# Linear attention with a relu feature map: the output product computed transposed, and turned back in fp32

## The chip, the cores and the metric

One core of a Trainium2 chip. The metric is the device time of the kernel in microseconds (us), the median of several runs. Smaller is better. All runs that are compared here were in the same (fast) state, with one exception that is named. Most runs of one kernel agree within about 0.3% (within 0.6% at most, but for one kernel that is named), so differences of half a per cent are read from five rounds with an interval.

TensorE is the matrix engine, VectorE and ScalarE work elementwise, GpSimd (POOL in the profile) and SyncE (SP) here mostly issue transfers. PE is TensorE's matmul part and PEld its weight loads, DVE is VectorE, ACT is ScalarE.

## The reference

```python
batch, heads, seq, dim = 8, 12, 512, 64          # Q, K, V: fp32
Q_feat = np.maximum(0, Q);  K_feat = np.maximum(0, K)
KV    = np.einsum('bhkd,bhkv->bhdv', K_feat, V)
K_sum = np.sum(K_feat, axis=2)
numerator   = np.einsum('bhqd,bhdv->bhqv', Q_feat, KV)
denominator = np.einsum('bhqd,bhd->bhq', Q_feat, K_sum)
return numerator / (denominator[:, :, :, None] + 1e-10)
```

There are 96 heads. The kernel takes K and V in 24 groups of four heads and Q in 12 octets of eight heads. A partition holds 16 (K, V) or 32 (Q, out) consecutive rows of 64 numbers, so every transfer of the body is contiguous. It must read 37.75 MB and write 12.58 MB.

## The kernel before

```python
def mm_kv(g):                       # KV and K_sum of one group: 16 matmuls
    ps_kv[g] = pkv.tile([P, 2, D1], fp32, name="ps_kv")
    for r in range(R):
        nc.tensor.matmul(ps_kv[g], kf[g][:, r, :, :]..., vo[g % NB][:, r, :, :], start=(r == 0), ...)

def evac_qt(o, i, eng=None):        # relu(q), transposed; written so that pairs of heads lie 32 columns apart
    for z in range(2):
        ... nc.scalar.activation(qtz[o % NZ][:, z, us, :, z, :], pv[:, :, :, z, :], Act.Relu)

def mm_out(o, j):                   # 128 small matmuls an octet: 32 columns of q as weights, 130 columns of KV
    ...                             # po: a PSUM tile for nu blocks of 128 rows, from block u0
    for v in range(nu):
        u, b, c = u0 + v, v // (nu // 2), v % (nu // 2) * 2 * D1
        for z in range(2):
            for w in range(4):
                hs, h = slice(32 * w, 32 * w + 32), 2 * w + z
                nc.tensor.matmul(po[hs, b, c:c + 2 * D1],
                    qtf[o % NZ][:, z, u * P + 32 * w:u * P + 32 * w + 32],
                    kvd[...][:, h % 4 // 2, h % 2, :, :], start=(z == 0), stop=(z == 1), ...)

def norm(o, j, o_sb):               # the denominator comes as column 64 of each row of the product
    ...                             # pv: a view of the product in PSUM; den and rec: small tiles
    nc.vector.tensor_scalar(den, pv[:, :, :, D], scalar1=1e-10, scalar2=None, op0=Alu.add)
    nc.vector.reciprocal(rec, den)
    nc.vector.tensor_tensor(o_sb[...], pv[:, :, :, 0:D], rec..., op=Alu.mult)

def cuts(o):                        # stores 1 and 3 are cut, so that engines 0 to 4 get more rows
    return ((16, P), (0, 5), (5, 10), (10, 15), (15, 16)) if o in (1, 3) else ((0, P),)

def store(o, o_sb):
    if o + DELAY < NO:              # hold store o back until K of a later octet has landed
        nc.sync.dma_start(out=scratch, in_=k_sb[2 * (o + DELAY)][0:1, 0, :])
    if o == NO - 1: ...             # the last octet's output in two halves
    for p0, p1 in cuts(o):
        nc.sync.dma_start(out=Ov[p0:p1], in_=o_sb[p0:p1])
# ... loads of Q, K, V are issued from GpSimd's queue and cast fp32 to bf16
```

## Time and profile before

| | before |
|---|---|
| time, median of 3 runs | 127.53 us (127.42 to 127.59) |
| span of the profiled run | 125.6 us |
| TensorE matmuls, weight loads | 2112, 2112 |
| last Q landed | 111.5 us |
| last store issued, landed | 119.9, 124.7 us |

Two more views of the kernel before matter later, though the prediction passed them by. The first is the list of transfer queues (queue and kind: packets, MB, and the time that its packets took as a share of the time of all 16 engines). The second lists what TensorE waited for (engine, tile and line, releaser: us in total, times, longest).

```profile
q0 software_dynamic: 8064, 17.83, 74.3%
q1 hardware_dynamic: 2416, 13.63, 27.1%
...
q8 instruction: 16, 0.26, 0.7%
```
```profile
PE ps_out L178 <- issue: 12.4, 7, 3.3
```

The first line of queues is the loads, the second the stores. The third is the program itself. Sixteen packets of 16 KB were read to feed instructions, and they went through the same DMA engines as the data. By the trace's packet records each took 0.88 to 0.98 us of one engine (0.94 us on average); their share of the time agrees (0.7% of 125.6 us, for 16 packets on 16 engines). The wait line is the other side of it: seven times TensorE stood for up to 3.3 us in the output product with no data to wait for. Three more such waits stand in TensorE's other lines. All ten (17.7 us together) end 1.2 to 1.5 us after one of these packets has been read, so they are waits for instructions.

### The profile page before, as it was taken

To read this page: it belongs to the slowest core of one execution; us is meant where nothing else is said; L and a number is where in the kernel's file an instruction comes from. 1 tells how busy PE (TensorE), PEld (TensorE's weight loads), DVE (VectorE), ACT (ScalarE), POOL (GpSimd) and SP (SyncE) were. 2 spreads that over 40 slices of the span, in tenths; PEclk is the share of its full clock that TensorE was granted. 3 is DMA by queue.
4 is the path that set the end of the run, shared out by engine and by line. 5 is a ranking of instruction groups with operands and counts; after the bars stand their busy time and mean duration, and the time that the engine had idled before them with its cause. 6 is when DMAs were issued, how large, how long until landed. Compare 5 with 4: busy or idle time off the path is not lost.

```text
span 125.6 us, 4876 instructions
## 1 busy us (share of the span) xinstructions
PE 78.7 (63%) x2112; PEld 69.4 (55%) x2112; DVE 81.2 (65%) x212; ACT 76.0 (61%) x167; POOL 31.7 (25%) x62
## 2 busy tenths in 40 slices
PE   0042908978398956535996697289765997558300
PEld 0041907957387845435985686287744895457200
DVE  3356785798936959674569697439628658942910
ACT  0255891599298898660899849509908959535000
POOL 6903334323243331241142133034022000000000
PEclk9999999999859999996799859959996579985995
DMA  3999999999999999999999999999999999999993
GB/s 120 378 305 210 217 204 211 217 207 219 202 215 211 208 217 320 260 216 311 270 211 296 290 211 281 296 221 231 343 223 215 328 258 213 322 419 417 407 400 153
DMA packets 10789, 32.82 MB, mean 261 GB/s; under 512 B 1424, under 2 KB 1424, under 8 KB 9360
## 3 DMA queue, kind: packets, MB, share of 16 engines
q0 software_dynamic: 8064, 17.83, 74.3%
q1 hardware_dynamic: 2416, 13.63, 27.1%
q10 hardware_dynamic: 288, 1.05, 2.1%
q8 instruction: 16, 0.26, 0.7%
q14 instruction: 5, 0.04, 0.1%
HBM read 37.75 MB, written 12.58 MB: 401 GB/s over the span
## 4 chain that ended last, share of the span: by engine, by line
DMA 32%; PE 30%; DVE 15%; issue 12%; ACT 6%; SPq 0%; ACTq 0%
DMA v_sb<-in_V_dram 25%; PE ps_out L178 14%; PE ps_kv L139 12%; DMA kv_first<-in_K_dram 7%; DVE o_sb L191 5%; PE ps_qt L153 4%; DVE kf L128 3%; DVE qt L121 3%; ACT qt L163 3%; ACT kvd L146 2%; DVE vo L130 2%; DVE rec L190 1%; ACT vo L134 1%; DVE den L188 1%; DVE kvd L118 0%
## 5 line engine op out<-in xcount | busy, mean ns | idle before, releaser
L139 PE MATMUL ps_kv<-vo,kf 128*128 128x130 bf16 x384 | 33.6, 253 | 22.2 <-ACT vo L134 10.1
L178 PE MATMUL ps_out<-kvd,qt 128*32 128x130 bf16 x1536 | 33.4, 240 | 16.1 <-issue 12.4
L139 PEld LDWEIGHTS <-kf 128*128 128x128 bf16 x384 | 28.6, 114 | 25.6 <-DVE vo L130 16.9
L178 PEld LDWEIGHTS <-qt 128*32 128x32 bf16 x1536 | 26.6, 106 | 21.6 <-issue 14.0
L146 ACT CAST kvd<-ps_kv 64x130 bf16<-64x130 f32 x96 | 25.2, 263 | 19.2 <-PE ps_kv L139 17.3
L134 ACT ACTIVATE vo<-v_sb,mask 128x1024 bf16<-128x1024 bf16 x22 | 26.2, 1190 | 10.9 <-DMA v_sb<-in_V_dram 10.7
L191 DVE TENSOR_TENSOR o_sb<-ps_out,rec 128x768 f32<-128x768 f32 (+1 forms) x36 | 31.3, 869 | 1.4
L163 ACT ACTIVATE qt<-ps_qt 128x512 bf16<-128x512 bf16 x46 | 23.8, 603 | 0.3
L128 DVE TENSOR_SCALAR kf<-k_sb,mask 128x1024 bf16<-128x1024 bf16 x44 | 19.1, 477 | 6.2 <-DMA k_sb<-in_K_dram 6.2
L85 POOL DMA_DIRECT2D k_sb<-in_K_dram x22 | 12.5, 569 | 39.5 <-DMA q_sb<-in_Q_dram 24.6
L188 DVE TENSOR_SCALAR den<-ps_out 128x12 f32<-128x12 f32 (+1 forms) x36 | 5.9, 164 | 17.8 <-PE ps_out L178 17.8
L153 PE MATMUL ps_qt<-ident,q_sb 128*128 128x128 bf16 x192 | 16.3, 251 | 1.2 <-issue 0.9
L87 POOL DMA_DIRECT2D v_sb<-in_V_dram x22 | 12.2, 555 | 16.3 <-DMA k_sb<-in_K_dram 6.7
L153 PEld LDWEIGHTS <-q_sb 128*128 128x128 bf16 x192 | 14.6, 116 | 1.4 <-issue 1.0
L130 DVE TENSOR_SCALAR vo<-v_sb,mask 128x1024 bf16<-128x1024 bf16 x22 | 10.7, 485 | 1.1 <-DMA v_sb<-in_V_dram 1.1
L190 DVE RECIPROCAL rec<-den 128x12 f32<-128x12 f32 (+1 forms) x36 | 7.9, 220 | 1.2
L91 POOL DMA_DIRECT2D q_sb<-in_Q_dram x12 | 6.5, 542 | 7.8 <-DMA v_sb<-in_V_dram 4.1
L128 DVE TENSOR_SCALAR kf<-kv_first,mask 128x1024 bf16<-128x1024 f32 x4 | 2.9, 766 | 4.6 <-DMA kv_first<-in_K_dram 4.6
L134 ACT ACT_TABLE_LOAD x1 | 1.3, 1283 | 5.5 <-DMA kv_first<-in_V_dram 5.5
L121 DVE MEMSET qt<- 128x2048 f32 x2 | 3.5, 1765 | 0.7 <-issue 0.7
L134 ACT ACTIVATE vo<-kv_first,mask 128x1024 bf16<-128x1024 f32 x2 | 2.4, 1179 | 2.7 <-DMA kv_first<-in_V_dram 2.7
L160 DVE TENSOR_SCALAR qt<-ps_qt 128x512 bf16<-128x512 bf16 x2 | 0.8, 420 | 2.9 <-PE ps_qt L153 2.9
(13 smaller groups left out, 4.9 us busy)
## 6 DMA issues: line engine op xcount, KB each, us to landing
out_dram<-o_sb SPq DMA_DIRECT2D x9, 1024.0 KB, 9.4
q_sb<-in_Q_dram POOLq DMA_DIRECT2D x12, 512.0 KB, 14.7
k_sb<-in_K_dram POOLq DMA_DIRECT2D x22, 256.0 KB, 14.0
v_sb<-in_V_dram POOLq DMA_DIRECT2D x22, 256.0 KB, 13.4
out_dram<-o_sb SPq DMA_DIRECT2D x2, 896.0 KB, 8.8
kv_first<-in_V_dram ACTq DMA_DIRECT2D x2, 512.0 KB
kv_first<-in_K_dram SPq DMA_DIRECT2D x2, 512.0 KB
out_dram<-o_sb SPq DMA_DIRECT2D x2, 512.0 KB, 4.7
```

What stands on the lines that cost most here:

```text
L85: nc.gpsimd.dma_start(out=k_sb[g].rearrange("p r d -> p (r d)"), in_=Kr[g])
L87: nc.gpsimd.dma_start(out=v_sb[g].rearrange("p r d -> p (r d)"), in_=Vr[g])
L128: nc.vector.tensor_scalar(kf[g][:, :, s, :], k_sb[g], scalar1=0.0, scalar2=mask[:, 0, s:s + 1], op0=Alu.max, op1=Alu.mult)
L130: nc.vector.tensor_scalar(vo[g % NB][:, :, 0, 0:D], v_sb[g], scalar1=mask[:, 1, 0:1], scalar2=None, op0=Alu.mult)
L134: nc.scalar.activation(vo[g % NB][:, :, 1, 0:D], v_sb[g], Act.Copy, scale=mask[:, 1, 1:2])
L139: nc.tensor.matmul(ps_kv[g], kf[g][:, r, :, :].rearrange("p s d -> p (s d)"), vo[g % NB][:, r, :, :], start=(r == 0), stop=(r == R - 1), s ...
L146: nc.scalar.copy(kvd[g % NK][64 * c:64 * c + 64, :, s, c, :], ps_kv[g][64 * s:64 * s + 64])
L153: nc.tensor.transpose(ps_qt[o, i][:, u, :], q_sb[o][:, i * (U // 2) + u, :], ident)
L163: nc.scalar.activation(qtz[o % NZ][:, z, us, :, z, :], pv[:, :, :, z, :], Act.Relu)
L178: nc.tensor.matmul(po[hs, b, c:c + 2 * D1], qtf[o % NZ][:, z, u * P + 32 * w:u * P + 32 * w + 32], kvd[(2 * o + h // 4) % NK][:, h % 4 // ...
L190: nc.vector.reciprocal(rec, den)
L191: nc.vector.tensor_tensor(o_sb[:, 2 * u0:2 * (u0 + nu)].rearrange("p (b r) d -> p b r d", b=2), pv[:, :, :, 0:D], rec.unsqueeze(3).to_broa ...
```

## The change

The intent is fewer and larger instructions. The output product is computed the other way round (KV as weights, q as the moving operand), eight matmuls of 256 columns in place of 128 small ones. That yields the output transposed. ScalarE (in the last octet VectorE too) copies it out of PSUM in fp32, and TensorE transposes it back in fp32. The denominators get 16 small matmuls of their own. Stores are no longer cut.

```diff
+    def out_t(o):
+        ...                             # q: relu(q), transposed, by heads
+        for j in range(2):
+            ps = pou.tile([P, 4, U, 16], fp32, name="ps_ot", tag="ps_out")
+            for i in range(4):
+                h = 4 * j + i
+                nc.tensor.matmul(ps[:, i], kvd[o % NK][:, h, 1:2 * D + 1], q[:, :, h, :], ...)
+            copy = nc.vector.tensor_copy if o == NO - 1 and j == 1 else nc.scalar.copy
+            copy(ot[o][:, :, 4 * j:4 * j + 4], ps.rearrange("p h u c -> p u h c"))
+    def denom(o):
+        ...                             # ps, own, den: tiles
+        for u in range(U):
+            nc.tensor.matmul(ps[:, u], qt_sb[o % NZ][:, u, :], kvd[o % NK][:, :, 0:2 * D1:2 * D1 - 1], ...)
+        nc.vector.scalar_tensor_tensor(own..., ps..., 1e-10, mask_h..., op0=Alu.add, op1=Alu.mult)
+        nc.vector.tensor_reduce(out=den..., in_=own..., op=Alu.add, ...)
+        nc.vector.reciprocal(rec[o], den)
+    def back(o, j):
+        for v in range(8):
+            nc.tensor.transpose(ps[:, 2 * v:2 * v + 2]..., ot[o][:, 8 * j + v]..., ident32)
+    def norm(o, j, ps, o_sb):
+        nc.vector.tensor_tensor(o_sb[:, rs], ps, rec[o][:, rs]..., op=Alu.mult)
-    def mm_out(o, j):  ...              # and the old norm
-        for p0, p1 in cuts(o):
-            nc.sync.dma_start(out=Ov[p0:p1], in_=o_sb[p0:p1])
+        nc.sync.dma_start(out=Ov, in_=o_sb)
     ... (half of the value copies move from ScalarE to VectorE, K/V of two groups share one
          evacuation, tiles and program order follow; mask_h is summed from the fp32 identity)
```

More of the change, by code (lines that the diff above doesn't have):

```diff
@@ L49 @@
     kfp = pool("kfp", 4)
-    rcp = pool("rcp", 4)
+    rcp = pool("rcp", 2)
     outp = pool("outp", DELAY + 2)
-    pkv = pool("pkv", 2, space=bass.MemoryType.PSUM)
+    otp = pool("otp", 2)
+    pkv = pool("pkv", 1, space=bass.MemoryType.PSUM)
     pqt = pool("pqt", 2, space=bass.MemoryType.PSUM)
+    pde = pool("pde", 1, space=bass.MemoryType.PSUM)
     pou = pool("pou", 2, space=bass.MemoryType.PSUM)
@@ L61 @@
     ident = consts.tile([P, P], bf16, name="ident")
+    ident32 = consts.tile([P, P], fp32, name="ident32")
     NB = 4
-    NK = 4
+    NK = 2
     NZ = 2
-    vo = [consts.tile([P, R, 2, D1], bf16, name=f"vo{i}") for i in range(NB)]
-    kvf = [consts.tile([P, NHG * 2 * D1], bf16, name=f"kvd{i}") for i in range(NK)]
-    kvd = [x.rearrange("p (t s c d) -> p t s c d", t=2, s=2, c=2) for x in kvf]
+    D4 = D + 4
+    vo = [consts.tile([P, R, 2, D4], bf16, name=f"vo{i}") for i in range(NB)]
+    kvf = [consts.tile([P, 8 * 2 * D1], bf16, name=f"kvd{i}") for i in range(NK)]
+    kvd = [x.rearrange("p (h d) -> p h d", h=8) for x in kvf]
     mask = consts.tile([P, 2, 2], fp32, name="mask")
     scratch = consts.tile([1, D], bf16, name="scratch")
-    qtf = [consts.tile([P, 2, U * P], bf16, name=f"qt{i}") for i in range(NZ)]
-    qtz = [x.rearrange("p z (u w y c) -> p z u w y c", u=U, w=4, y=2) for x in qtf]
+    mask_h = consts.tile([P, 8, 2], fp32, name="mask_h")
+    qt_sb = [consts.tile([P, U, P], bf16, name=f"qt{i}") for i in range(NZ)]
+    ps_kv = pkv.tile([P, 2, 256], fp32, name="ps_kv")
     ctx.enter_context(tc.manual_schedule())
@@ L113, in zero, with zero_kv @@
                 nc.vector.memset(mask[64 * t:64 * t + 64, 1, t:t + 1], 1.0)
-        if i < NB:
-            nc.vector.memset(vo[i][:, :, :, D:D1], 0.0)
-            for t in range(2):
-                nc.vector.memset(vo[i][64 * t:64 * t + 64, :, t, D:D1], 1.0)
+        ones = vo[i][:, :, :, 1:D4 - 1]
+        nc.vector.memset(ones[:, :, :, 0:D + 2:D1], 0.0)
+        for t in range(2):
+            nc.vector.memset(ones[64 * t:64 * t + 64, :, t, 0:D + 2:D1], 1.0)
+    def zero_kv(i):
         nc.vector.memset(kvf[i].bitcast(fp32), 0.0)
-    def zero_q(i):
-        nc.vector.memset(qtf[i].rearrange("p z f -> p (z f)").bitcast(fp32), 0.0)
-    kf, ps_kv, ps_qt, ps_out = {}, {}, {}, {}
+    kf, ot, rec = {}, {}, {}
     def prep(g):
@@ L129, in prep, with prep_v @@
                                     scalar2=mask[:, 0, s:s + 1], op0=Alu.max, op1=Alu.mult)
-        nc.vector.tensor_scalar(vo[g % NB][:, :, 0, 0:D], v_sb[g], scalar1=mask[:, 1, 0:1],
+        nc.vector.tensor_scalar(vo[g % NB][:, :, 0, 2:D + 2], v_sb[g], scalar1=mask[:, 1, 0:1],
                                 scalar2=None, op0=Alu.mult)
-    def prep_act(g):
-        nc.scalar.activation(vo[g % NB][:, :, 1, 0:D], v_sb[g], Act.Copy, scale=mask[:, 1, 1:2])
+    def prep_v(g, eng):
+        if eng is nc.scalar:
+            nc.scalar.activation(vo[g % NB][:, :, 1, 2:D + 2], v_sb[g], Act.Copy, scale=mask[:, 1, 1:2])
+        else:
+            nc.vector.tensor_scalar(vo[g % NB][:, :, 1, 2:D + 2], v_sb[g], scalar1=mask[:, 1, 1:2],
+                                    scalar2=None, op0=Alu.mult)
@@ L136, in mm_kv, with evac_kv @@
     def mm_kv(g):
-        ps_kv[g] = pkv.tile([P, 2, D1], fp32, name="ps_kv")
         for r in range(R):
             nc.tensor.matmul(
-                ps_kv[g], kf[g][:, r, :, :].rearrange("p s d -> p (s d)"), vo[g % NB][:, r, :, :],
+                ps_kv[:, g % 2, 0:2 * (D + 2)].rearrange("p (t d) -> p t d", t=2),
+                kf[g][:, r, :, :].rearrange("p s d -> p (s d)"), vo[g % NB][:, r, :, 1:D4 - 1],
                 start=(r == 0), stop=(r == R - 1), skip_group_check=True)
-    def evac_kv(g):
+    def evac_kv(o, gs):
@@ L144, in evac_kv @@
         for s in range(2):
             for c in range(2):
-                nc.scalar.copy(kvd[g % NK][64 * c:64 * c + 64, :, s, c, :],
-                               ps_kv[g][64 * s:64 * s + 64])
-    def transp(o, i):
-        ps_qt[o, i] = pqt.tile([P, U // 2, P], bf16, name="ps_qt")
-        for u in range(U // 2):
-            nc.tensor.transpose(ps_qt[o, i][:, u, :], q_sb[o][:, i * (U // 2) + u, :], ident)
-    def evac_qt(o, i, eng=None):
-        us = slice(i * (U // 2), (i + 1) * (U // 2))
-        pv = ps_qt[o, i].rearrange("p u (w y c) -> p u w y c", w=4, y=2)
-        for z in range(2):
-            if eng is nc.vector:
-                eng.tensor_scalar(qtz[o % NZ][:, z, us, :, z, :], pv[:, :, :, z, :], scalar1=0.0,
-                                  scalar2=None, op0=Alu.max)
-            else:
-                nc.scalar.activation(qtz[o % NZ][:, z, us, :, z, :], pv[:, :, :, z, :], Act.Relu)
@@ L166 @@
-    ROUNDS = ((0, 6), (6, 6), (12, 4))
-    def mm_out(o, j):
-        po = pou.tile([P, 2, 512], fp32, name="ps_out")
-        ps_out[o, j] = po
-        u0, nu = ROUNDS[j]
-        for v in range(nu):
-            u, b, c = u0 + v, v // (nu // 2), v % (nu // 2) * 2 * D1
-            for z in range(2):
-                for w in range(4):
-                    hs = slice(32 * w, 32 * w + 32)
-                    h = 2 * w + z
-                    nc.tensor.matmul(
-                        po[hs, b, c:c + 2 * D1],
-                        qtf[o % NZ][:, z, u * P + 32 * w:u * P + 32 * w + 32],
-                        kvd[(2 * o + h // 4) % NK][:, h % 4 // 2, h % 2, :, :],
-                        start=(z == 0), stop=(z == 1), skip_group_check=True)
@@ L184, in norm @@
-    def norm(o, j, o_sb):
-        u0, nu = ROUNDS[j]
-        pv = ps_out[o, j][:, :, 0:nu * D1].rearrange("p b (r d) -> p b r d", d=D1)
-        den = rcp.tile([P, 2, nu], fp32, name="den")
-        nc.vector.tensor_scalar(den, pv[:, :, :, D], scalar1=1e-10, scalar2=None, op0=Alu.add)
-        rec = rcp.tile([P, 2, nu], fp32, name="rec")
-        nc.vector.reciprocal(rec, den)
-        nc.vector.tensor_tensor(
-            o_sb[:, 2 * u0:2 * (u0 + nu)].rearrange("p (b r) d -> p b r d", b=2),
-            pv[:, :, :, 0:D],
-            rec.unsqueeze(3).to_broadcast([P, 2, nu, D]), op=Alu.mult)
@@ L198, in cuts, with qt @@
-    def cuts(o):
-        return ((16, P), (0, 5), (5, 10), (10, 15), (15, 16)) if o in (1, 3) else ((0, P),)
+                nc.scalar.copy(
+                    kvd[o % NK][64 * c:64 * c + 64, 4 * gs.start + s:4 * gs.stop:2,
+                               c * D1:c * D1 + D1].rearrange(
+                        "p (g t) d -> p g t d", t=2),
+                    ps_kv[64 * s:64 * s + 64, gs, 0:2 * (D + 2)].rearrange(
+                        "p g (t d) -> p g t d", t=2)[:, :, :, c:c + D1])
+    def qt(o):
+        for i in range(2):
+            us = slice(i * (U // 2), (i + 1) * (U // 2))
+            ps = pqt.tile([P, U // 2, P], bf16, name="ps_qt")
+            for u in range(U // 2):
+                nc.tensor.transpose(ps[:, u, :], q_sb[o][:, i * (U // 2) + u, :], ident)
+            if o == NO - 1 and i == 1:
+                nc.vector.tensor_scalar(qt_sb[o % NZ][:, us], ps, scalar1=0.0, scalar2=None,
+                                        op0=Alu.max)
+            else:
+                nc.scalar.activation(qt_sb[o % NZ][:, us], ps, Act.Relu)
@@ new lines, in out_t @@
+    def out_t(o):
+        ot[o] = otp.tile([P, U, 8, 16], fp32, name="ot_sb")
+        q = qt_sb[o % NZ].rearrange("p u (h c) -> p u h c", h=8)
+        for j in range(2):
+            ps = pou.tile([P, 4, U, 16], fp32, name="ps_ot", tag="ps_out")
+            for i in range(4):
+                h = 4 * j + i
+                nc.tensor.matmul(ps[:, i], kvd[o % NK][:, h, 1:2 * D + 1], q[:, :, h, :],
+                                 start=True, stop=True, skip_group_check=True)
+            copy = nc.vector.tensor_copy if o == NO - 1 and j == 1 else nc.scalar.copy
+            copy(ot[o][:, :, 4 * j:4 * j + 4], ps.rearrange("p h u c -> p u h c"))
@@ new lines, in denom @@
+    def denom(o):
+        ps = pde.tile([P, U, 8, 2], fp32, name="ps_den")
+        for u in range(U):
+            nc.tensor.matmul(ps[:, u], qt_sb[o % NZ][:, u, :], kvd[o % NK][:, :, 0:2 * D1:2 * D1 - 1],
+                             start=True, stop=True, skip_group_check=True)
+        own = rcp.tile([P, U, 8, 2], fp32, name="own")
+        nc.vector.scalar_tensor_tensor(
+            own.rearrange("p u h c -> p u (h c)"), ps.rearrange("p u h c -> p u (h c)"), 1e-10,
+            mask_h.rearrange("p h c -> p (h c)").unsqueeze(1).to_broadcast([P, U, 16]),
+            op0=Alu.add, op1=Alu.mult)
+        den = rcp.tile([P, RQ], fp32, name="den")
+        nc.vector.tensor_reduce(out=den.rearrange("p (u c) -> p u c", c=2),
+                                in_=own.rearrange("p u h c -> p u c h"), op=Alu.add,
+                                axis=mybir.AxisListType.X)
+        rec[o] = rcp.tile([P, RQ], fp32, name="rec")
+        nc.vector.reciprocal(rec[o], den)
@@ new lines, in back @@
+    def back(o, j):
+        ps = pou.tile([P, 16, D], fp32, name="ps_bk", tag="ps_out")
+        for v in range(8):
+            nc.tensor.transpose(ps[:, 2 * v:2 * v + 2].rearrange("p c d -> p (c d)"),
+                                ot[o][:, 8 * j + v].rearrange("p h c -> p (h c)"), ident32)
+        return ps
+    def norm(o, j, ps, o_sb):
+        rs = slice(16 * j, 16 * j + 16)
+        nc.vector.tensor_tensor(o_sb[:, rs], ps,
+                                rec[o][:, rs].unsqueeze(2).to_broadcast([P, 16, D]), op=Alu.mult)
@@ L212, in store @@
             return
-        for p0, p1 in cuts(o):
-            nc.sync.dma_start(out=Ov[p0:p1], in_=o_sb[p0:p1])
-    zero(0)
-    prep(0)
-    prep_act(0)
-    zero(1)
-    prep(1)
-    prep_act(1)
-    zero_q(0)
-    for k in range(2, NK):
-        zero(k)
-    zero_q(1)
-    def kv(g):
-        mm_kv(g)
-        evac_kv(g)
-    def qt(o):
-        for i in range(2):
-            transp(o, i)
-            evac_qt(o, i, nc.vector if o == NO - 1 and i == 1 else None)
-    def prepare(g):
-        prep(g)
-        prep_act(g)
@@ L239, in out_round @@
-    def out_round(o, j, o_sb):
-        mm_out(o, j)
-        norm(o, j, o_sb)
-    for o in range(NO + 1):
-        if o > 0:
-            o_sb = outp.tile([P, RQ, D], fp32, name="o_sb", tag="o_sb")
-        if o < NO - 1:
-            kv(2 * o)
-        if o > 0:
-            out_round(o - 1, 0, o_sb)
-        if o < NO - 2:
-            prepare(2 * o + 2)
-        if o > 0:
-            out_round(o - 1, 1, o_sb)
-        if o < NO - 1:
-            kv(2 * o + 1)
-            qt(o)
-        if o < NO - 2:
-            prepare(2 * o + 3)
-        if o > 0:
-            out_round(o - 1, 2, o_sb)
-            store(o - 1, o_sb)
-        if o == NO - 2:
-            prepare(2 * NO - 2)
-        if o == NO - 1:
-            prepare(2 * NO - 1)
-            kv(2 * NO - 2)
-            kv(2 * NO - 1)
-            qt(o)
+        nc.sync.dma_start(out=Ov, in_=o_sb)
@@ new lines, in out_tile @@
+    def out_tile():
+        return outp.tile([P, RQ, D], fp32, name="o_sb", tag="o_sb")
+    both = slice(0, 2)
+    for g in range(2):
+        zero(g)
+        prep(g)
+        prep_v(g, nc.scalar)
+    nc.vector.tensor_copy(ident32, ident)
+    for c in range(2):
+        nc.vector.tensor_reduce(out=mask_h[:, :, c], in_=ident32.rearrange("p (h b) -> p h b", h=8),
+                                op=Alu.add, axis=mybir.AxisListType.X)
+    for k in range(NK):
+        zero_kv(k)
+    for g in range(2, NB):
+        zero(g)
@@ new lines, with backs, kvs @@
+    mm_kv(0)
+    evac_kv(0, slice(0, 1))
+    mm_kv(1)
+    evac_kv(0, slice(1, 2))
+    qt(0)
+    def backs(o):
+        o_sb = out_tile()
+        for j in range(2):
+            norm(o, j, back(o, j), o_sb)
+        store(o, o_sb)
+    def kvs(o):
+        mm_kv(2 * o)
+        mm_kv(2 * o + 1)
+        evac_kv(o, both)
+    SAME = NO - 4
+    for o in range(NO - 2):
+        if 0 < o <= SAME:
+            kvs(o)
+        prep(2 * o + 2)
+        prep_v(2 * o + 2, nc.scalar)
+        if 0 < o <= SAME:
+            backs(o - 1)
+        denom(o)
+        out_t(o)
+        prep(2 * o + 3)
+        prep_v(2 * o + 3, nc.vector)
+        if o >= SAME:
+            kvs(o + 1)
+        qt(o + 1)
+        if o >= SAME:
+            backs(o)
@@ L272 @@
+    o = NO - 2
+    g = 2 * NO - 2
+    prep(g)
+    prep_v(g, nc.vector)
+    denom(o)
+    out_t(o)
+    mm_kv(g)
+    evac_kv(o + 1, slice(0, 1))
+    prep(g + 1)
+    prep_v(g + 1, nc.vector)
+    backs(o)
+    mm_kv(g + 1)
+    evac_kv(o + 1, slice(1, 2))
+    qt(o + 1)
+    out_t(o + 1)
+    denom(o + 1)
+    backs(o + 1)
 _INS = ['Q', 'K', 'V']
```

## The prediction

> **What bounds the kernel now.** I read the page first (busy shares, slices), then the busy time by stretches, then the chain of work that ended last, then the times to landing of the last load and the last store, and last the groups by shape, for durations.
>
> ```profile
> PE 78.7 (63%) x2112; PEld 69.4 (55%) x2112; DVE 81.2 (65%) x212; ACT 76.0 (61%) x167; POOL 31.7 (25%) x62
> ...
> DMA  3999999999999999999999999999999999999993
> ```
>
> No compute engine passes 65%, while the DMA row is full from the second slice to the last but one. The stretches say the same (last two columns: DMA share and GB/s, counted at the destination):
>
> ```profile
> 3.00:43.00 40.00, 25.09 (x583) 22.61 (x584) 27.80 (x67) 26.32 (x56) 14.98 (x28) 0.96 1.09 232
> 43.00:103.00 60.00, 43.41 (x1193) 38.39 (x1191) 41.12 (x101) 41.60 (x95) 14.82 (x27) 0.86 1.09 262
> 103.00:111.50 8.50, 4.83 (x187) 3.79 (x185) 6.92 (x18) 5.98 (x13) 0.00 (x0) 1.00 1.08 292
> 111.50:119.00 7.50, 5.41 (x159) 4.59 (x156) 3.52 (x10) 2.14 (x6) 0.00 (x0) 0.77 1.00 421
> 119.00:124.00 5.00, 0.00 (x0) 0.00 (x0) 0.82 (x2) 0.00 (x0) 0.00 (x0) 0.86 0.89 365
> ```
>
> A casting load reads 4 bytes for each 2 it writes, so 232 GB/s of mostly loads is about 420 GB/s on the HBM side, which is what the pure stores reach at the end (421). The page counts 37.75 MB read and 12.58 MB written: 50.33 MB at 420 GB/s is 119.8 us. The span is 125.6 us, and about 2.5 us of that is start-up and 1 us is drain. So the DMA engines are the bound, and only 2 or 3 us of the span could be had by anyone. The last load and the last store:
>
> ```profile
> L91 POOL DMA_DIRECT2D q_sb<-in_Q_dram x1: 527/527/527, 95.1 to 95.1; - x1
> ...
> DMA to landing us min/median/max: 16.4/16.4/16.4
> ```
> ```profile
> L211 SPq DMA_DIRECT2D out_dram<-o_sb x1: 333/333/333, 119.9 to 119.9; - x1
> ...
> DMA to landing us min/median/max: 4.8/4.8/4.8
> ```
>
> The last Q lands at 95.1 + 16.4 = 111.5 us; the last half octet of output is issued at 119.9 and lands at 124.7. Between them the engines are full of stores held back on purpose (store o waits for a K load ten groups ahead). The last octet's arithmetic therefore has 8.4 us beside the stores, and it uses all of it:
>
> ```profile
> 111.26 1.12 PE ps_kv L139 x16
> ...
> 113.61 1.09 ACT qt L163 x2
> ...
> 114.75 1.29 PE ps_out L178 x35
> ...
> 119.17 0.69 DVE o_sb L191
> ```
>
> The DMA share falls to 0.89 only after 119, so this tail is just in time, with perhaps 1 us of slack: a later last store shows nearly one for one once the backlog is out.
>
> **What the Trainium skill says.** "Perfetto Trace Analysis", Roofline, caps one core at its 16 DMA engines, about 435 GB/s; the 420 here agrees. "TensorE: Matmul & The Clock Gate", Terms, says that transpose_mode is 4x faster for FP32, and its Weight-path table that fast weight load excludes FP32; no fp32 transpose is in the trace, so this is the open number of the case. "DMA: Bandwidth & Descriptors", the section on why a DMA increments its semaphore by 16, says that a DMA spreads over the largest k up to 16 that divides its outer dimension, on the hardware queues the lowest-numbered engines. By that, the cuts (rows 16 to 128, then 5, 5, 5 and 1 rows) leave seven rows of 8 KB to all 16 engines and give three more to engines 0 to 4; the profile names no engine, so no run here shows it.
>
> **The change, part by part.** Durations by shape, from the trace of before:
>
> ```profile
> L146 ACT CAST kvd<-ps_kv 64x130 bf16<-64x130 f32 x96 | 25.2, 263 | 19.2 <-PE ps_kv L139 17.3
> L163 ACT ACTIVATE qt<-ps_qt 128x512 bf16<-128x512 bf16 x46 | 23.8, 603 | 0.3
> L191 DVE TENSOR_TENSOR o_sb<-ps_out,rec 128x768 f32<-128x768 f32 x24 | 23.0, 957 | 1.0
> L191 DVE TENSOR_TENSOR o_sb<-ps_out,rec 128x512 f32<-128x512 f32 x12 | 8.3, 692 | 0.4
> ```
>
> TensorE, one octet at full clock. Before: two key-value products (16 matmuls in 1.04 us each in the chain), 16 transposes in 0.89, 128 output matmuls at about 16.5 ns (x92 in 1.52): 5.1 us. After: the 128 go (-2.1). Eight matmuls of 256 columns come: at the 65 ns of a 130-column one, 8 x 128 ns = 1.0. Sixteen 16-column denominator matmuls, paced by their weight loads like the transposes: 0.9. Sixteen fp32 transposes back: unknown. One pass like bf16 would be 0.06 us each, plus the slower weight load; four passes above 0.3. I choose 0.15 to 0.2, so 2.4 to 3.2. Sum 7.3 to 8.1 us.
>
> ScalarE over the whole kernel: the q evacuations become 23 of 1024 columns (603 + 512 x 0.83 = 1.03 us, 23.7, unchanged). Copies of the transposed output come: 23 x 1.03 = +23.7. Twelve of 24 value copies move to VectorE: 12 x 1.19 = -14.3. In ten octets eight casts of 130 become four of 260 (263 + 108 = 0.37): -6. Total 76 + 3 = 79 us.
>
> VectorE: norm with its two small operations was 31.3 + 5.9 + 7.9 = 45.1. After: the two forms give 265 ns for 256 columns, so 1024 take 1.22 us, 24 of them 29.3; twelve times a masked add, a reduce and a reciprocal of about 1.0 (my estimate from 256 elements at that slope, plus overheads): 12. Value copies +12 x 0.485 = 5.8; the two zero fills of q go, -3.5; the last copy +1.2; head mask, fp32 identity and further fills about +1, at the start beside the first loads. Total near 82 us.
>
> Per octet that is TensorE 8, ScalarE and VectorE 7 us. The stream gives 7.5 us an octet before stores begin and 10.0 after, on average (111.5 - 13) / 11 = 9 us. So the middle stays under the loads and costs nothing.
>
> The tail, after V of the last group at 107.4 (ScalarE waits for it until 107.5): program order puts both transposes back of octet 10, sixteen of them, ahead of the last key-value product on TensorE. With 0.11 us each I get: product done at 111.6, q transposed at 112.5, relu until 113.8, eight output matmuls until 114.8, VectorE's copy until 116.0, its three denominator operations until 117.0, transposes back beside them, then two norms of 1.22: last store issued at 119.5, like before. With 0.2 us each, octet 9's and octet 10's transposes push the last product to 114.1 and the chain gives 123.1, 3 us later; issue plus the shortest landing I believe in, 3.5 us, is 126.6, two more than before.
>
> The cuts of stores 1 and 3 go. If they relieve eleven engines of two rows of 8 KB, their loss costs 16 KB at 26 GB/s, 0.6 us, where the slowest engine ends the run; I take 0.3.
>
> **Rivals.** (a) Nothing shows: transfers hide all and the time stays at 127.5. For it: full DMA in every slice. Against: the 1 us of slack in the tail. (b) TensorE becomes the bound: at 0.35 us a transpose an octet takes 10.5 us, above the 9 us of the stream, and twelve octets end near 13 + 126 + 4, over 140 us. Against: transpose mode is said to cost less; for it: the granted clock was 0.86 from 43 to 103 us, which stretches 8 us to 9.3. (c) The shorter engine work makes the tail earlier: then the floor of 50.33 MB keeps the gain under about 1 us, 126.5 at best.
>
> **Range and chances.** The middle term is 127.5, plus 0.3 for the cuts, plus 0.7 for a tail between the two chains: 128.5. A one-pass transpose gives 127.2 to 127.8; 0.2 us gives 129.5; slower transposes or half clock in the tail go past 130.1. I put 0.75 on within 2%, 0.23 on slower, and 0.02 on faster, for which the bytes leave no room. Eight times in ten between 127.0 and 131.0.
>
> **What would show it.** Right: DMA row full to slice 38; the last Q landing within 1 us of 111.5; fp32 transposes of 0.11 to 0.2 us pitch; the last store issued between 119.5 and 123. Wrong: Q landing late or gaps in the DMA row before 119 (TensorE holds the stream back); a last store earlier than 119 with an end that moves with it; transposes of 0.3 us or more; or output copies well above 1.03 us, since they read one order and write another.

## The result, and the profile after

| | before | after |
|---|---|---|
| time, median | 127.48 us, 6 runs (127.42 to 127.59) | 126.81 us, 6 runs (126.53 to 127.20) |
| TensorE matmuls, weight loads | 2112, 2112 | 1056, 1056 |
| last Q landed | 111.5 us | 110.35 us |
| last store issued, landed | 119.9, 124.7 us | 121.4, 124.0 us |

The ratio is 0.9949 (95% interval 0.9931 to 0.9966). Ratios here are the mean time of one kernel's fast runs over that of the other's of the same rounds, so not quite the ratio of the medians. This is a gain of half a per cent that the interval bears out, where the prediction expected a loss of 0.8%.

The page of the changed kernel, busy times, the DMA row and the queues:

```profile
PE 86.0 (69%) x1056; PEld 78.7 (63%) x1056; DVE 81.6 (65%) x175; ACT 78.9 (63%) x115; POOL 31.3 (25%) x62
...
DMA  3999999999999999999999999999999999999984
...
q0 software_dynamic: 8064, 17.83, 74.6%
q1 hardware_dynamic: 2384, 13.63, 27.2%
...
q8 instruction: 8, 0.13, 0.4%
```

The loads and stores move the same bytes and the DMA row is as full as before. TensorE is busier (86.0 us against 78.7), with half the instructions. One line changed in the change's favour: eight instruction packets instead of sixteen.

The groups of the added work (line, engine, operation, tiles, count | busy us, mean ns | idle before):

```profile
L221 DVE TENSOR_TENSOR o_sb<-ps_bk,rec 128x1024 f32<-128x1024 f32 x24 | 28.4, 1220 | 16.7 <-PE ps_bk L215 16.7
...
L215 PE MATMUL ps_bk<-ident,ot_sb 128*128 128x128 f32 x192 | 24.5, 284 | 1.1 <-DVE ot_sb L190 1.1
L190 ACT COPY ot_sb<-ps_ot 128x1024 f32<-128x1024 f32 x23 | 23.0, 1013 | 2.9 <-PE ps_ot L187 2.0
...
L200 DVE SCALAR_TENSOR_TENSOR own<-ps_den,mask_h 128x256 f32<-128x256 f32 x12 | 5.0, 416 | 3.3 <-PE ps_den L197 3.3
```

The mean of 284 ns of a transpose is its length in the pipeline, not its pace. Its pace is 24.5 / 192 = 0.128 us over the whole run, and the chain tells it by stage. Here is the end of the chain (start us, us, what):

```profile
109.22 1.75 PE ps_bk L215 x16
110.97 0.96 PE ps_kv L148 x16
...
113.07 1.03 ACT qt L176
114.10 0.04 issue
114.14 1.05 PE ps_ot L187 x8
...
115.28 1.23 DVE ot_sb L190
116.51 0.14 issue
116.65 3.47 PE ps_bk L215 x16
120.12 0.02 issue
120.14 1.23 DVE o_sb L221
```

Sixteen transposes take 1.75 us (0.109 each) in octet 10 and 3.47 us (0.217 each) in octet 11, where the granted clock was 0.55 on average (1.00 in octet 10's). Because of that the last store was issued 1.5 us later than before, yet the run ended earlier. The landing of the last store and the last stretches (PE, PEld, DVE, ACT, POOL busy with counts, granted clock, DMA share, GB/s) show how:

```profile
L234 SPq DMA_DIRECT2D out_dram<-o_sb x2: 332/332/332, 119.9 to 121.4; - x2
...
DMA to landing us min/median/max: 2.6/2.7/2.8
```
```profile
103.00:111.50 8.50, 6.98 (x88) 6.34 (x86) 7.32 (x14) 5.84 (x11) 0.00 (x0) 1.00 1.07 305
111.50:119.00 7.50, 5.11 (x58) 4.86 (x56) 4.81 (x8) 3.09 (x6) 0.00 (x0) 0.82 1.01 424
119.00:124.00 5.00, 1.11 (x7) 0.86 (x5) 2.08 (x2) 0.00 (x0) 0.00 (x0) 0.84 0.77 316
```

The last store found the DMA engines free and landed in 2.6 us, where the same store took 4.8 us before. The share between 119 and 124 us is 0.77, where it was 0.89. So the engines had less work left at that time, although the bytes are the same and the last Q came 1.1 us sooner. The question is what freed them.

### The profile page after: what moved, and what is told of

It reads as the page before. It is cut to its first block, busy times and chain, and to the rows that moved or that the text cites. A ratio compares the mean times of both kernels' runs of the same rounds, so it can differ in the third digit from the quotient of the medians.

```text
span 124.9 us, 2637 instructions
## 1 busy us (share of the span) xinstructions
PE 86.0 (69%) x1056; PEld 78.7 (63%) x1056; DVE 81.6 (65%) x175; ACT 78.9 (63%) x115; POOL 31.3 (25%) x62
## 4 chain that ended last, share of the span: by engine, by line
DMA 34%; PE 28%; DVE 26%; ACT 6%; issue 2%; SPq 0%; DVEq 0%; ACTq 0%; POOLq 0%
DMA v_sb<-in_V_dram 14%; DMA q_sb<-in_Q_dram 13%; DVE o_sb L221 12%; PE ps_kv L148 11%; PE ps_bk L215 8%; DMA kv_first<-in_K_dram 7%; PE ps_qt L171 5%; DVE kf L134 4%; ACT qt L176 4%; PE ps_ot L187 3%; ACT kvd L157 2%; DVE vo L136 2%; DVE vo L143 2%; DVE den L205 1%; DVE rec L209 1%
## 5 line engine op out<-in xcount | busy, mean ns | idle before, releaser
L148 PE MATMUL ps_kv<-vo,kf 128*128 128x132 bf16 x384 | 31.0, 246 | 17.9 <-ACT vo L141 8.2
L221 DVE TENSOR_TENSOR o_sb<-ps_bk,rec 128x1024 f32<-128x1024 f32 x24 | 28.4, 1220 | 16.7 <-PE ps_bk L215 16.7
L157 ACT CAST kvd<-ps_kv 64x260 bf16<-64x260 f32 (+1 forms) x56 | 19.2, 342 | 18.8 <-PE ps_kv L148 16.1
L176 ACT ACTIVATE qt<-ps_qt 128x1024 bf16<-128x1024 bf16 x23 | 22.4, 1026 | 6.7 <-PE ps_qt L171 6.6
L215 PE MATMUL ps_bk<-ident,ot_sb 128*128 128x128 f32 x192 | 24.5, 284 | 1.1 <-DVE ot_sb L190 1.1
L190 ACT COPY ot_sb<-ps_ot 128x1024 f32<-128x1024 f32 x23 | 23.0, 1013 | 2.9 <-PE ps_ot L187 2.0
L215 PEld LDWEIGHTS ps_bk<-ident,ot_sb 128*128 128x128 f32 x192 | 22.4, 149 | 1.1 <-ACT ot_sb L190 1.1
L187 PE MATMUL ps_ot<-qt,kvd 128*128 128x256 bf16 x96 | 14.5, 283 | 5.6 <-DVE o_sb L221 4.3
L187 PEld LDWEIGHTS <-kvd 128*128 128x128 bf16 x96 | 9.3, 100 | 8.2 <-issue 6.1
L141 ACT ACTIVATE vo<-v_sb,mask 128x1024 bf16<-128x1024 bf16 x10 | 11.5, 1154 | 0.2
```

Source lines behind the costliest of these rows:

```text
L148: nc.tensor.matmul(ps_kv[:, g % 2, 0:2 * (D + 2)].rearrange("p (t d) -> p t d", t=2), kf[g][:, r, :, :].rearrange("p s d -> p (s d)"), vo[ ...
L157: nc.scalar.copy(kvd[o % NK][64 * c:64 * c + 64, 4 * gs.start + s:4 * gs.stop:2, c * D1:c * D1 + D1].rearrange("p (g t) d -> p g t d", t=2 ...
L176: nc.scalar.activation(qt_sb[o % NZ][:, us], ps, Act.Relu)
L187: nc.tensor.matmul(ps[:, i], kvd[o % NK][:, h, 1:2 * D + 1], q[:, :, h, :], start=True, stop=True, skip_group_check=True)
L190: copy(ot[o][:, :, 4 * j:4 * j + 4], ps.rearrange("p h u c -> p u h c"))
L215: nc.tensor.transpose(ps[:, 2 * v:2 * v + 2].rearrange("p c d -> p (c d)"), ot[o][:, 8 * j + v].rearrange("p h c -> p (h c)"), ident32)
```

## The experiments

**The theory.** Every load and store is spread over 16 DMA engines and is done when the slowest of them is. An instruction fetch is 16 KB on one engine, so it makes that engine late, and whatever waits for that engine late with it. Half the TensorE instructions mean half the fetches. **Rivals:** (1) the cuts that were dropped had been a cost; (2) the shorter TensorE or ScalarE work in the tail gives the gain; (3) only the sum of bytes counts, and 0.13 MB of 50 is nothing.

All medians, with five rounds each; before was 127.48 to 127.51 us in these batches. "Wrong" marks a result that is wrong on purpose.

| kernel | us | ratio to before (95%) |
|---|---|---|
| before, no cuts | 128.03 | 1.0037 (1.0019 to 1.0055) |
| before, z=1 output matmuls left out (wrong) | 127.56 | 1.0000 (0.9981 to 1.002) |
| before, no cuts, 16 output matmuls an octet (wrong) | 126.64 | 0.9935 (0.9922 to 0.9947) |
| the same, with cuts (wrong) | 127.56 | 1.0006 (0.9994 to 1.0019) |
| after, again | 126.75 | 0.9943 (0.9931 to 0.9956) |
| after, cuts put back | 127.67 | 1.0006 (0.999 to 1.0023) |
| after, cut of store 1 alone | 127.30 | 0.9984 (0.9971 to 0.9996) |
| after, store 1 cut at rows 8 and 16 | 127.09 | 0.9972 (0.9958 to 0.9986) |
| after, TensorE kept warm in the tail | 126.78 | 0.9946 (0.9932 to 0.9959) |
| after, 1024 matmul pairs more | 142.95 | 1.1112 (1.1058 to 1.1166) |
| after, two 16 KB reads more | 126.67 | 0.9934 (0.9921 to 0.9948) |
| after, four 16 KB reads more | 127.70 | 1.0018 (1.0005 to 1.003) |

### The cuts, in both kernels

```diff
-        return ((16, P), (0, 5), (5, 10), (10, 15), (15, 16)) if o in (1, 3) else ((0, P),)
+        return ((0, P),)
```

> The kernel before with every store in one piece (the cuts of stores 1 and 3 removed, nothing else). My prediction's step (the cuts help): 0.3 us slower, 127.8 us. Rival, the cuts cost time and their loss is the gain of the change: 0.4 to 0.7 us faster, about 126.9, and the last Q lands near 110.4 us as in the changed kernel, not at 111.5. Third, the cuts do nothing: within 0.15 us of 127.5.

```diff
-        nc.sync.dma_start(out=Ov, in_=o_sb)
+        cuts = ((16, P), (0, 5), (5, 10), (10, 15), (15, 16)) if o in (1, 3) else ((0, P),)
+        for p0, p1 in cuts:
+            nc.sync.dma_start(out=Ov[p0:p1], in_=o_sb[p0:p1])
```

> The changed kernel with the cuts of stores 1 and 3 put back. If the cuts help: 126.5 us or less. If they cost: 127.2 or more, last Q near 111.5 us. If they do nothing: within 0.15 us of 126.8.

The kernel before loses 0.5 us without its cuts (128.03), and the changed kernel loses 0.9 us with them (127.67). So the cuts are no cost as such: they helped where they were tuned and hurt after the change. Rival 1 falls. Dropping them was worth a loss to the old kernel, and the rest of the change must be worth about 1.2 us (128.03 - 126.81).

The trace records each of the sixteen completions of a transfer. These are those of the last Q and of the last half octet of output, sorted, in us (not a view of the page, but the records of the completions):

```
before              out  122.6 122.7 122.8 123.8 124.0 124.1 124.1 124.2 124.2 124.3 124.3 124.4 124.6 124.6 124.6 124.7
before, no cuts     Q    107.6 107.7 107.7 107.7 107.9 108.0 108.7 108.9 109.4 109.5 110.7 110.8 111.2 111.5 112.0 112.1
                    out  122.9 123.0 123.0 123.0 123.1 123.5 123.5 123.6 124.6 124.7 124.9 125.0 125.2 125.2 125.3 125.3
after (first run)   Q    107.7 107.8 107.8 107.8 108.2 108.4 108.4 108.9 109.4 109.6 109.6 110.1 110.1 110.2 110.3 110.3
                    out  123.8 123.8 123.9 123.9 123.9 123.9 123.9 123.9 123.9 123.9 123.9 123.9 124.0 124.0 124.0 124.0
after (second run)  Q    107.9 108.0 108.0 108.0 108.3 108.6 108.9 109.0 109.2 109.7 109.8 110.3 110.4 110.4 110.4 111.0
                    out  122.4 122.7 122.8 123.0 123.0 123.1 123.2 123.5 123.6 123.8 123.9 123.9 123.9 124.0 124.1 124.2
after, cuts back    out  123.0 123.0 123.0 123.0 123.1 123.1 123.1 123.1 123.2 123.2 123.4 124.0 124.1 124.3 124.4 124.9
```

The early engines bring Q at the same 107.6 to 107.9 in both kernels. The late ones are 4.5 us behind them in the kernel before without cuts, 2.6 and 3.2 after the change. It is the late half that the change improved, not the pace. In the store of the kernel before without cuts the engines fall into eight early and eight late ones, 1 us apart, which is what the cuts were there to even out.

The counts of late engines fit one picture. Sixteen fetches without cuts make eight late. Eight fetches with cuts make five late (the last row). Sixteen fetches with cuts leave three early and thirteen late (the first row). That is 8 + 5 + 3 = 16, as if the fetches went round eight engines and the cuts loaded five of the others. The packet times of the kernel before point the same way, since they nearly repeat after eight: 935, 974, 975, 962, 879, 893, 949, 935 ns, then 935, 964, 974, 961, 894, 893, 934, 931. The profile names no engine, so this picture is argued and not shown.

### The number of TensorE instructions alone

The kernel before without cuts, with one full-width output matmul for each 128 rows in octets 0 to 8 in place of eight small ones. Nothing else of the change is in it. It leaves out 9 x 16 x 7 = 1008 matmuls and as many weight loads, and the result is wrong.

```diff
+            if o <= 8:
+                nc.tensor.matmul(po[:, b, c:c + 2 * D1], qtf[o % NZ][:, 0, u * P:u * P + P],
+                                 kvd[2 * o % NK][:, 0, 0, :, :], start=True, stop=True, ...)
+                continue
```

> The kernel before without cuts, and in octets 0 to 8 one full-width output matmul in place of eight narrow ones (wrong result on purpose), octets 9 to 11 as they were: 2016 fewer TensorE instructions, 8 fetches of 16 KB in place of 16, every other engine's work and all tensor traffic unchanged. Theory of the fetch (each 16 KB packet sets one DMA engine back, and the slowest engine ends the run): last Q at 110.4 to 110.8 us instead of 112.06, the two groups of engines that stood 1.3 us apart at the end come together, last landing near 124.0, time 126.5 to 126.9, as the changed kernel though nothing else of the change is in it. Rival (the gain comes from the new output path on ScalarE, VectorE or TensorE): 127.8 to 128.1, as without cuts before.

> The same with the cuts of stores 1 and 3 as in the kernel before. Theory of the fetch: the cuts now load engines that are not behind, one lands its last share 1.8 us and four 1.1 us after the rest, as with the cuts in the changed kernel: 127.4 to 127.8 us, slower than without. Rival (the cuts help whatever the fetches do): 126.4 or less.

Both times came as the theory has it: 126.64 us without cuts, 127.56 us with them. In the first the two groups of engines are gone (the last store's completions run from 122.2 to 124.2 us without a gap), in the second five engines end 0.8 to 1.5 us after the other eleven. The page of the first (its TensorE line and its instruction queue):

```profile
PE 72.7 (58%) x1104; PEld 65.1 (52%) x1104; DVE 80.5 (64%) x212; ACT 76.1 (61%) x167; POOL 32.2 (26%) x62
...
q8 instruction: 8, 0.13, 0.4%
```

With TensorE at 72.7 us it lands where the changed kernel lands with 86.0 us. So nothing else of the change (transposed output, copies, order of the program) is needed for the gain. The last Q landed at 110.7 us, and 112.1 us with the sixteen fetches. The four corners:

| | 16 fetches | 8 fetches |
|---|---|---|
| with cuts | 127.5 (before) | 127.6 (few matmuls), 127.7 (after with cuts) |
| without cuts | 128.0 (before without cuts) | 126.6 (few matmuls), 126.8 (after) |

A first try had been less clean. It left out half of the output matmuls and kept the cuts:

```diff
-            for z in range(2):
+            for z in range(2 if o > 8 else 1):
     ...                                # and stop=True on the half that stays
```

> The kernel before with the second half of the output matmuls left out in octets 0 to 8 (wrong result on purpose): 1152 fewer TensorE instructions, 4 or 5 fewer 16 KB fetches, about 1 us an octet less TensorE time in the middle, octets 9 to 11 as they were. Theory of the fetch: the last Q 0.3 to 0.6 us earlier than 111.5, time 127.0 to 127.3. Rival: no change, 127.5 within 0.15 us.

It gave 127.56 us, no gain with 12 fetches. That was a miss for the theory as I had put it, in which fewer fetches always help. The table above mends it: with cuts made for sixteen fetches, fewer of them gain nothing.

### Fetches added to the changed kernel

```diff
+        if 1 <= o <= 8:
+            for n in range(2):
+                for u in range(U):
+                    for w in range(4):
+                        nc.tensor.matmul(ps[hs, u], qt_sb[o % NZ][:, u, hs], kvd[...], start=True, stop=True, ...)
```

> The changed kernel with 1024 more small matmul pairs on TensorE (each denominator of octets 1 to 8 computed twice more, in 32-column pieces, into the tile that the real ones then overwrite; the result stays right). About 2 us an octet of TensorE time in the middle, which the 10 us stream should hide, and 2048 more instructions. Theory of the instruction fetch (16 KB packets on the DMA engines, 16 in the kernel before, 8 in the changed one): 16 such packets again, the last Q about 0.5 to 1.1 us later than 110.35, time up by 0.3 to 0.7 us, to 127.1 to 127.5. Rival (the fetches lie beside the other packets for nothing): last Q within 0.3 us, time within 0.2 us of 126.8.

It took 142.95 us and missed every expectation. (Three of its six runs, the profiled one among them, count as slow against its fastest, 140.74 us; the ratio uses the other three. The step is far larger than that.) What TensorE waited for in it, and its DMA row:

```profile
PE ps_den L201 <- issue: 10.6, 3, 4.0
PE ps_kv L148 <- ACT vo L141: 8.3, 1, 8.3
PE ps_qt L171 <- issue: 5.5, 2, 2.9
```
```profile
DMA  4999999999999999999999999999999971071524
```

The added matmuls, and the stalls at their fetches (up to 4.0 us each), made TensorE the bound: the DMA row breaks off and TensorE works on alone. In one respect it agrees with the theory. With 16 fetches the last Q landed at 112.0 us, as in the kernel before without cuts, though all but TensorE's added work is that of the changed kernel. As a test of the total it is useless, because two causes were changed at once.

### 16 KB on one engine, without TensorE

A cleaner test leaves TensorE's program alone. A read of one row of 4093 fp32 elements is put in the queue of the loads, so that it can't be cut into sixteen. "DMA: Bandwidth & Descriptors" of the Trainium skill, in the section on why a DMA increments its semaphore by 16, gives such a prime length to one engine, and successive ones in GpSimd's queue to successive engines. The runs below don't bear out the second half.

```diff
+        if o in (3, 6):                 # the other kernel: (2, 4, 6, 8)
+            nc.gpsimd.dma_start(out=junk[0][:, 0:4093], in_=<4093 elements of K, one row>)
```

> The changed kernel with two needless reads of one row of 16 KB (4093 fp32 elements) in the queue of the loads, in octets 3 and 6; TensorE's program is untouched. Slowest-engine theory: 16 KB given to one DMA engine cost what a fetch of instructions costs, 0.6 to 0.9 us on that engine, and stores and loads wait for the slowest engine: 127.4 to 128.4 us (the lower end if the two go to different engines). Rival, only the sum of bytes counts: 32 KB of 50.33 MB is 0.06%, 0.08 us, so 126.7 to 126.9 us.

> The same with four such reads, in octets 2, 4, 6 and 8. Slowest-engine theory, all on one engine: 2.4 to 3.6 us above the changed kernel, 129 to 130.5 us; each on another engine: about 0.6 to 0.9 us, 127.4 to 127.8 us. Sum of bytes: +0.15 us, 126.8 to 127.0 us.

Two reads cost nothing (126.67 us), a miss for the theory's lower end. Four cost 0.9 to 1.0 us (127.70 against 126.75 and 126.67), six times the 0.15 us that the bytes are worth. Rival 3 falls with the four. The number lies inside the range written down for four different engines, but the trace speaks against that branch. It records each read as one packet of 0.62 us, so on four engines they would set each back by 0.62 us. The last Q of that run, in its sixteen completions:

```
four reads more     Q    107.5 107.5 107.6 107.7 108.1 108.1 108.2 108.2 108.9 108.9 109.2 109.2 109.2 109.3 109.9 112.2
```

Fifteen engines had their share by 109.9, one came 2.3 us later, and the transfer is done when that one is. That is close to 4 x 0.62 = 2.5 us, as if all four reads had gone to one engine. For one engine I had written down 2.4 to 3.6 us more, and the end moved by 1.0. So the range that was met was met by luck. Two reads (1.25 us) on an engine that is early anyway would be free, and that would explain the two. Which engine got what the profile does not tell, so this part is argued, not shown.

### The tail

```diff
+    warm(<scratch in PSUM>, 16)        # idle matmuls after the last transposes of q
     out_t(o + 1)
     denom(o + 1)
+    warm(<scratch in PSUM>, 12)        # and ahead of the last transposes back
     backs(o + 1)
```

> The changed kernel with 28 idle-time matmuls in the last octet (16 after q is transposed, 12 after the denominators, into PSUM that nobody reads) so that the granted clock does not drop to 0.5 during the last 16 transposes back. If the tail of arithmetic now ends the run: transposes 1.75 us instead of 3.47, the last store issued near 120.2 instead of 121.4, last landing 123.4 to 123.8, time 126.2 to 126.6. If the DMA engines still end it: the store is earlier but the landing stays at 124.0, time 126.8 within 0.15.

The timeline of its tail (start us, us, engine, line, operation):

```profile
115.51 1.94 PE L215 MATMUL ps_bk<-ident,ot_sb 128*128 128x128 f32 x16 [0.34 <-DVE ot_sb L190]
...
117.88 1.46 SPq L234 DMA_DIRECT2D out_dram<-o_sb  x2
```

The transposes ran at full clock, and the last store was issued at 119.0 us instead of 121.4. The time is 126.78 us, no gain: the store then took 5.0 us to land. The unchanged kernel, run again, showed the same by chance:

> The changed kernel once more, beside the same runs of the kernel before: 126.8 us within 0.2, last Q within 0.4 us of 110.35, and the last store landing on all 16 engines within 0.3 us. If the last Q moves by a microsecond between two runs of one kernel, single profiles can't carry the argument.

In this second profile the last store was issued at 119.0 us too, and it landed at 124.2, against 124.0 for a store issued 2.4 us later in the first profile. Rival 2 falls: the tail's arithmetic has about 2 us of play and does not set the time. My expectation that its sixteen completions would stay within 0.3 us was a miss (1.8 us, as listed above). They had been that close in the first profile only because the late store found all engines idle. The last Q was a second miss: it came at 111.0 us, 0.7 us later than in the first profile and not within 0.4. So the last Q of a single profile is good to about 0.7 us. The profiles without cuts keep apart all the same: 110.3 to 111.0 us in five with eight fetches (after twice, kept warm, two reads more, few matmuls), 112.0 and 112.1 us in the two with sixteen.

### Other cuts for the changed kernel

```diff
+        cuts = ((16, P), (0, 5), (5, 10), (10, 15), (15, 16)) if o == 1 else ((0, P),)
+        cuts = ((16, P), (0, 8), (8, 16)) if o == 1 else ((0, P),)        # the other kernel
```

> The changed kernel with the cut of store 1 alone put back (two rows of 8 KB more for engines 0 to 4 in place of all, and one more for the first). Slowest-engine theory: half of what the two cuts cost (0.9 us), so 127.1 to 127.4 us, unless engines 0 to 4 are those that are early with eight fetches, then about 126.5 us. Rival, the extra stores cost only their issue: 126.8 us.

> The changed kernel with store 1 cut into rows 16 to 128, 0 to 8 and 8 to 16: eight engines get one row of 8 KB (0.3 us) more, the other eight one fewer. Slowest-engine theory: between 126.5 us (the eight are early) and 127.2 us (they are late). Rival, only the number of stores matters: as the run with the cut of store 1 alone.

Both lose, by 0.5 us (127.30) and 0.3 us (127.09). With 0.9 us for both old cuts, the loss grows with the number of extra stores (2, 4, 8) as well as with the rows they shift, so these two runs don't tell a cost per store from imbalance. That cuts aren't simply a cost is known from the kernel before alone. No version was found that beats the changed kernel by more than the noise.

## Why the prediction was wrong, point by point

- **The bound: right.** The DMA row stayed full, and the middle of the run cost nothing although TensorE's work rose by 7 us. The "Roofline" ceiling of "Perfetto Trace Analysis" in the Trainium skill (about 435 GB/s for 16 engines) held: 424 GB/s in the stores at the end. Of the signs named for this, the DMA row was full to slice 38, but the last Q came 1.1 us before 111.5, just outside the 1 us allowed.
- **Durations: right.** Output copies 1.013 us (predicted 1.03), relu 1.026 (1.03), norm 1.220 (1.22). ScalarE came to 78.9 us (79) and VectorE to 81.6 (82). The three denominator operations took 0.42 + 0.42 + 0.35 = 1.19 us (about 1.0), and the 16 denominator matmuls 0.58 us in the timeline (0.9).
- **The transposes: the first branch was right.** The pitch is 0.109 us at full clock, the 0.11 of the first chain, not the 0.15 to 0.2 that I chose. At half clock it is 0.217 us, which did occur in the last octet.
- **Step that failed, "plus 0.7 for a tail between the two chains": it was worth nothing.** The last store was indeed late in the first profile (121.4 us), and the end did not move with it: it landed at 124.0 us, and at 124.2 when it was issued at 119.0. "Just in time, with perhaps 1 us of slack" had mistaken DMA engines that end late for a tail that ends late. The shortest landing, put at 3.5 us, was 2.6 us.
- **Step that failed, "plus 0.3 for the cuts": the wrong sign in this kernel.** It is a loss of 0.5 us in the kernel before, as argued, but the cuts fit sixteen fetches and the changed kernel has eight. There they would have cost 0.9 us.
- **The missing term: instruction fetches.** The prediction counted 4224 TensorE instructions becoming 2112 only as TensorE time. By the two kernels without cuts the rest of the change is worth -1.2 us, and the kernel with fewer matmuls and nothing else has all of it (-1.4 us). The sum 127.5 + 0.5 - 1.2 + 0 gives 126.8, the measured time, but only because the -1.2 is its remainder; with the -1.4 of the other kernel it is 126.6.
- **Rivals.** (a) "Nothing shows" was nearest, and (c) named the right floor, 126.5 at best, for a wrong reason: not a shorter tail but engines that end more evenly. (b), TensorE as the bound, was wrong for this kernel; the run with 1024 more matmul pairs shows how it looks.

What stays open: a fetch has two effects, an engine made late and a TensorE that stands still. The four extra reads leave TensorE's program alone and show that the first can move the end by about 1 us, and the runs of the tail show that TensorE had play there. In the kernels with cuts, TensorE's standing for instructions fell from 17.7 us (before) to 1.8 us with twelve fetches and to nothing with eight, and none of the three was faster (127.56 to 127.67 us). So with the cuts in, less standing bought nothing. Without cuts both effects change together (20.9 us of standing with sixteen fetches, 0.3 us or none with eight), and how much of the 1.2 us each contributes was not separated. If the fetches do go round eight engines, eight fewer free 0.94 us on each (an estimate from the packet times), which would not cover the 1.2 to 1.4 us alone.

## What to carry to other kernels

When the DMA engines are the bound, count the instructions too: TensorE's program comes in 16 KB packets through the same engines, and a transfer waits for the slowest of them. A hand-made balance of transfers belongs to one program; when the instruction count changes, measure it again. And a last store that is issued late is not yet a late end: look at how long it takes to land.

## What the Trainium skill lacked or had wrong

- "Advanced Engine Details and Errata", ISA Cache, states a line of 16 KB for 256 instructions; the runs agree (4224 TensorE instructions in 16 packets of 16 KB, 2112 in 8). "Runtime: NRT & Kernel Launch", Instruction fetch mechanics, gives the fetch a DMA queue of its own and calls its cost mostly hidden. Here it was not hidden: TensorE stood still for up to 3.3 us at a time in the kernel before (4.0 us in the run with more matmul pairs). Both lack that each packet takes a DMA engine from the data for about 0.94 us.
- "DMA: Bandwidth & Descriptors", the section on the semaphore increment of 16, says that sixteen engines finish independently. It lacks how far apart they drift under a full load: 4.5 us for one Q load of the kernel before without cuts, 2.6 and 3.2 us in two profiles after the change.
- "TensorE: Matmul & The Clock Gate", Terms, calls transpose mode 4x faster for FP32 and gives no time for FP32. Here a 128x128 fp32 transpose had a pitch of 109 ns at full clock and 217 ns at a mean granted clock of 0.55, a bf16 one 56 ns (16 in 0.89 us).
- The same page, PE-mode transpose, says that the full clock does not engage for transpose mode. Read as "transposes never run at the full clock" that is wrong here: sixteen fp32 transposes ran at a granted clock of 1.00 behind a matmul group (1.75 us in the chain, 1.91 in the timeline, which counts the last one's length too), and at 1.00 with idle matmuls ahead of them (1.94 us in the timeline). After TensorE had waited they took 3.47 us at 0.55. Whether transposes alone can raise the clock no run shows.
- No page has the landing time of a half-megabyte store in SyncE's queue on idle engines (the fit in "DMA: Bandwidth & Descriptors" is for GpSimd's queue): 2.6 us here, against 4.8 to 5.2 us behind other stores.
